# Sending values and keys through DRAM whole, and splitting them where a head loads them

## The chip, the cores and the metric

The kernel runs on one core of a Trainium2 chip. A core has a matrix engine (TensorE, PE in the profile; its weight loads are PEld), a vector engine (VectorE, DVE), an activation engine (ScalarE, ACT), a general engine (GpSimd, POOL) and a queue engine that issues most transfers (SyncE, SP). Each engine works through its own list of instructions in order and waits on semaphores; 16 DMA engines move data between the on-chip memory (SBUF, 128 partitions) and DRAM. Matrix products land in PSUM. The metric is device microseconds of one launch.

## What is computed

Two layers of an encoder with 1024 tokens of width 1024, all in float32. Each layer normalises its input, projects it with one matrix `w_in`, and splits the columns among four groups of four attention heads; their outputs are concatenated, projected with `w_out` and added back; then comes an MLP with squared ReLU.

```python
for l in range(DEPTH):                                  # 2 layers
    h = rms_norm(x, norm1_g[l]);  proj = h @ w_in[l]
    y_a = mla_mixer(...)     # A: 4 heads, dense, latent q and kv, key 64 + 32 rotary
    y_b = diff_mixer(...)    # B: 4 heads, dense, difference of two softmaxes
    y_c = swa_mixer(...)     # C: 4 query heads on 2 key heads, window of +-128 tokens
    y_d = na_mixer(...)      # D: 4 heads, neighbourhood of 8 rows x 16 columns, bias rpb
    x = x + concat(norms of y_a, y_b, y_c, y_d) @ w_out[l]
    x = x + square(relu(rms_norm(x, norm2_g[l]) @ w_up[l])) @ w_down[l]
```

In D the tokens form a grid of 16 rows by 64 columns. A query sees 8 rows and 16 columns around it, and each pair adds a bias from the table `rpb`. All heads have 64 value columns.

## The kernel before

**Precision.** TensorE multiplies the type fp32r. To keep float32 accuracy an operand is held as two fp32r parts: `hi`, a rounded copy that ACT writes (`nc.scalar.activation(hi, src, AF.Copy)`, line L196 in `split`), and `lo = src - hi`, written by DVE or POOL (`tt`, L190). A product then takes several passes over the parts (L222, L223, L224 for the projections).

**Stages of a layer.** `attention` first runs the projections of B in two waves, then four attention stages in the order B, D, C, A. Within a stage `weave` places other products between the attention steps as filler: the projections of A's latents and of D while B runs, the projections of C and A's up-projections (`latent_up`) while D runs, and early parts of the output projection (`groups_bd`) while C and A run. The MLP follows, with a hand-written PE order.

**Through DRAM.** Projected queries, keys and values have tokens and features in the wrong places for attention, so the evacuations store them to DRAM tensors (`keep`, L169, on the SP queue), and each head loads its own (`load`, L162, on SP as well). Before the change every one of these tensors holds both parts. `emit_parts` splits a projected block (ACT copy, subtraction on POOL or DVE) into the tile `both` (two buffers) and stores it; `to_values` transposes a block of values on PE into PSUM, and writes `hi` with ACT (L646) and `lo` with DVE (L190) into `both`. The DRAM tensors are `vb`, `vd`, `vc`, `va` for values (each token row 64 hi and 64 lo), `kd` and `kc` for the keys of D and C (two parts), and others for queries and for the keys of A and B.

**Loading a head.** `vtile` loads one head's values, 512 KB, straight into the tile `v` (two buffers). In `attn_d` a head loads its bias (six blocks of 128 x 128, one buffer), the query parts into one stack tile, and the key parts into two: part hi into both halves of `ks[0]`, part lo into both halves of `ks[1]`, four transfers of 256 KB. `attn_c` does the same once for each of the two key heads. The stack tiles come from the pool `xp` with eight buffers. The softmax tiles `p` (128 x 1024, tag "p") have six buffers (`NP`).

**Attention steps.** For B and A, `softmax` computes scores of a query block (L810), DVE finds the row minimum of the negated scores (L812), ACT exponentiates (L815); B adds the two softmaxes with ACT (L898) and POOL. `dense` transposes the probabilities (L846), splits them (L196, L190 into `pth`, `ptl`) and multiplies with `v` (L834, L835). For D and C, `banded` does the same with blocks of three key tiles: scores L982, `finish` (L1058 and L1061 in D, L1089 and L1092 in C), transposes L991, products L1003 and L1004. `neighbours` builds, once on the host, the index from which a D head's bias blocks are gathered.

**Ending a head.** `denominators` sends the row sums through DRAM (`drows`) and loads them spread over partitions (`rz`); `times` multiplies, and `mix_group` normalises the group and splits it into `mix` tiles, from which the filler `groups_bd` can start. That filler first loads four tiles `sum` of 512 KB.

**What sets the order.** The program text gives priorities (`tc.high_priority`, `weave`); a planner then fixes, before anything runs, one order per engine and the buffer of each tile, from its own estimates of the durations. A change of a load or a buffer can therefore move many neighbouring instructions. At run time each engine keeps that order. SP's transfers use eight semaphores in turn, and in much of the order a transfer waits for the one eight places ahead of it to land.

Of the kernel before, what the change touches and what calls it, by code (L numbers as in the profile page):

```python
# [21 lines left out]
P = 128  # L22
# [56 lines left out]
def neighbours():  # L79
# [8 lines left out]
    out = np.full((P, 6, P), -1)  # L88
    for slot, ok in enumerate((row_ok & (ck >= c), row_ok, row_ok & (ck < c), row_ok, row_ok, row_ok)):
        at = (rk - r + 7) * 31 + 8 * (slot % 3 - 1) + ck - c + 15  # L90
        out[:, slot] = np.where(np.broadcast_to(ok, (P, P)), at, -1)
# [56 lines left out]
class Trunk:  # L148
# [232 lines left out]
    def attention(self, l):  # L381
# [8 lines left out]
        qb, kb, vb = dr([2, 2, 4, 16, 2, S], "qb"), dr([2, 2, 4, 16, 2, S], "kb"), dr([4, P, 8, P], "vb")  # L390
        qd, kd, vd = dr([2, 2, P, S], "qd"), dr([2, 2, P, S], "kd"), dr([4, P, 8, P], "vd")
        qc, kc, vc = dr([2, 2, 2, 32, 2, S], "qc"), dr([2, 2, 32, 2, S], "kc"), dr([2, P, 8, P], "vc")
        lat, krd = dr([2, 3, P, S], "lat"), dr([2, 16, 2, S], "krd")
        qa = dr([2, 2, P, S], "qan"), dr([2, 4, 16, 2, S], "qar")
        ka, va = dr([2, 2, P, S], "kan"), dr([4, P, 8, P], "va")
# [13 lines left out]
        def proj_d():  # L409
            for t in range(2):  # L410
                yield from one(T_DQ[t], xs, self.ev_grid(rb, self.to_parts(qd[:, t], 0.125)))
                yield from one(T_DK[t], xs, self.ev_grid(rb, self.to_parts(kd[:, t])))
# [177 lines left out]
    def ev_rope(self, tabs, dst):  # L590

        dst = dst.rearrange("a g f h s -> a (g f) h s")

        def ev(n, ps):
# [6 lines left out]
            self.tt(t1, t1, t2, ALU.add, self.eng)  # L601
            self.emit_parts(t1, [(dst[:, :, h, sl].rearrange("a p s -> p a s"), slice(h * 64, h * 64 + 64))
# [31 lines left out]

    def to_values(self, dst, tag="mm"):
# [3 lines left out]
        def then(n, y):  # L639
# [3 lines left out]
            src = ps.rearrange("p (k h d) -> p h k d", k=4, h=2)  # L643
            b = self.both()
            v = b.rearrange("p h (k e) -> p h k e", k=4)
            nc.scalar.activation(v[..., 0:64], src, AF.Copy)  # L646
            self.tt(v[..., 64:128], src, v.bitcast(F)[..., 0:64], ALU.subtract)
            self.keep(dst[:, :, n * 4:n * 4 + 4].rearrange("h p k e -> p h (k e)"), b.bitcast(F))
# [143 lines left out]

    def vtile(self, src):
        v = self.ap.tile([P, 8, P], R, tag="v", bufs=2, name="v")
        self.load(v.bitcast(F), src)
        return v
# [238 lines left out]
    def attn_d(self, l, qd, kd, vd, ys):  # L1035
        nc = self.nc
        for t in range(2):
            y, rz = self.ypair(), self.rz_tile()
            for h2 in range(2):
                h = 2 * t + h2  # L1040
                bias = self.ap.tile([P, 6, P], F, tag="bias", bufs=1, name="bias")
# [3 lines left out]
                for i in range(2):  # L1045
                    half = slice(i * 64, (i + 1) * 64)
                    self.load(qs.bitcast(F)[half], qd[i, t, rows])
                    self.load(ks[0].bitcast(F)[half], kd[0, t, rows])
                for i in range(2):
                    self.load(ks[1].bitcast(F)[i * 64:(i + 1) * 64], kd[1, t, rows])  # L1050
# [448 lines left out]
```

## Time and profile before

| | us |
|---|---|
| median of 3 runs | 2708.47 (2705.57 to 2710.37) |
| the profiled execution | 2709.95 |
| its span, first to last instruction | 2707.9 |
| PE busy | 2549.6 (94%) |
| DVE busy | 1943.0 (72%) |
| ACT busy | 1439.8 (53%) |
| POOL busy | 1130.9 (42%) |
| moved by DMA | 389.19 MB, mean 144 GB/s |

The profile page gives one execution, cut into 40 equal slices, with the busy share of each engine, the clock that was granted to TensorE and the share of the DMA engines. The first layer's attention lies between 0 and about 620 us, its MLP up to about 1390 us; the second layer's attention from there to about 1980 us. In layer 0 the first query block of B is exponentiated at 89 us, the first scores of D are at 330 us, and C and A follow until the MLP. Other views used below: the busy time of each engine in chosen stretches, groups of like instructions with their mean duration, who waited for whom, the instructions in order of time, and the chain of work that ended last.

### The profile page before, as it was taken

To read this page: it belongs to the slowest core of one execution; us is meant where nothing else is said; L and a number is where in the kernel's file an instruction comes from. 1 tells how busy PE (TensorE), PEld (TensorE's weight loads), DVE (VectorE), ACT (ScalarE), POOL (GpSimd) and SP (SyncE) were. 2 spreads that over 40 slices of the span, in tenths; PEclk is the share of its full clock that TensorE was granted. 3 is DMA by queue.
4 is the path that set the end of the run, shared out by engine and by line. 5 is a ranking of instruction groups with operands and counts; after the bars stand their busy time and mean duration, and the time that the engine had idled before them with its cause. 6 is when DMAs were issued, how large, how long until landed. Compare 5 with 4: busy or idle time off the path is not lost.

```text
span 2707.9 us, 37502 instructions
## 1 busy us (share of the span) xinstructions
PE 2549.6 (94%) x12296; PEld 2112.5 (78%) x12296; DVE 1943.0 (72%) x3379; ACT 1439.8 (53%) x2601; POOL 1130.9 (42%) x754
## 2 busy tenths in 40 slices
PE   8989988999899998999999999889998999999997
PEld 6778876787778887888877788668876788878886
DVE  6777866774966668887567777677749666688775
ACT  4667756664534444444436776566635344444444
POOL 2555642201345554545434656321013455544442
PEclk9989988999999999999998899899999999999998
DMA  5534597222144457444244446962221444664431
GB/s 175 169 107 129 158 287 239 82 89 63 46 144 148 153 170 267 143 142 141 95 139 134 121 113 183 295 202 69 71 71 52 154 153 152 221 221 146 136 105 63
DMA packets 186931, 389.19 MB, mean 144 GB/s; under 512 B 23712, under 2 KB 26736, under 8 KB 186736
## 3 DMA queue, kind: packets, MB, share of 16 engines
q1 hardware_dynamic: 172912, 361.62, 43.2%
q10 hardware_dynamic: 13824, 25.17, 2.7%
q8 instruction: 97, 1.59, 0.2%
q14 instruction: 98, 0.80, 0.1%
HBM read 263.29 MB, written 123.41 MB: 143 GB/s over the span
## 4 chain that ended last, share of the span: by engine, by line
PE 73%; DVE 12%; DMA 6%; ACT 4%; issue 3%; POOL 1%; SPq 0%; DVEq 0%; ACTq 0%; POOLq 0%
PE u L222 8%; PE u L224 8%; PE u L223 8%; PE mm L222 5%; PE mm L223 5%; PE mm L224 5%; PE p L222 5%; PE p L223 5%; PE p L224 5%; PE sb L810 3%; PE tr L846 3%; DVE p L812 2%; DVE part L190 2%; PE pv L835 2%; PE pv L834 2%
## 5 line engine op out<-in xcount | busy, mean ns | idle before, releaser
L190 POOL TENSOR_TENSOR wl<-raw,wh 128x512 fp32r<-128x512 f32 x448 | 632.8, 1413 | 704.8 <-ACT wh L196 691.0
L196 ACT ACTIVATE wh<-raw 128x512 fp32r<-128x512 f32 x448 | 281.5, 629 | 576.2 <-PE u L223 310.9
L190 POOL TENSOR_TENSOR wl<-ws,wh 128x512 fp32r<-128x512 f32 (+1 forms) x112 | 147.3, 1316 | 461.0 <-ACT wh L196 436.1
L222 PE MATMUL u<-far,wh 128*128 128x512 f32 x768 | 301.8, 393 | 11.4 <-ACT ev L1242 8.3
L224 PE MATMUL u<-far,wl 128*128 128x512 f32 x768 | 300.6, 391 | 2.2 <-POOL wl L190 2.2
L190 DVE TENSOR_TENSOR raw<-raw 128x512 f32<-128x512 f32 x256 | 223.1, 877 | 109.1 <-POOL wl L190 55.6
L223 PE MATMUL u<-far,wh 128*128 128x512 f32 x768 | 300.6, 391 | 0.0
L190 DVE TENSOR_TENSOR ptl<-tr,pth 128x512 fp32r<-128x512 f32 (+2 forms) x384 | 238.3, 629 | 68.5 <-ACT pth L196 66.8
L815 ACT ACTIVATE p<-p,nm 128x1024 f32<-128x1024 f32 x192 | 220.2, 1147 | 92.3 <-DVE nm L812 91.6
L196 ACT ACTIVATE pth<-tr 128x512 fp32r<-128x512 f32 (+2 forms) x384 | 205.2, 546 | 108.5 <-PE tr L846 64.9
L222 PE MATMUL p<-far,wh 128*128 128x512 f32 x640 | 252.9, 395 | 7.5 <-DVE ev L190 7.5
L224 PE MATMUL p<-far,wl 128*128 128x512 f32 x640 | 251.5, 393 | 1.5 <-POOL wl L190 1.5
L223 PE MATMUL p<-far,wh 128*128 128x512 f32 x640 | 252.2, 394 | 0.0
L810 PE MATMUL sb<-stack 96*128 96x512 f32 x640 | 217.5, 422 | 22.1 <-DVE nm L812 21.4
L190 DVE TENSOR_TENSOR far<-act,far 128x512 fp32r<-128x512 f32 x224 | 207.3, 955 | 14.7 <-ACT far L196 14.7
L190 POOL TENSOR_TENSOR p<-p 128x1024 f32<-128x1024 f32 x64 | 154.0, 2411 | 129.6 <-ACT p L898 121.3
L222 PEld LDWEIGHTS u<-far,wh 128*128 128x128 f32 x768 | 145.3, 189 | 43.5 <-ACT ev L1242 9.1
L222 PE MATMUL mm<-xh,wh 128*128 128x512 f32 x416 | 170.9, 411 | 0.8 <-DVE part L190 0.3
L224 PEld LDWEIGHTS u<-far,wl 128*128 128x128 f32 x768 | 145.2, 189 | 33.5 <-POOL wl L190 3.0
L812 DVE CUSTOM_DVE_ANT_0 p<-sb,zero,nm 128x512 f32<-128x512 f32 x192 | 142.4, 743 | 37.7 <-PE sb L810 34.6
L223 PEld LDWEIGHTS u<-far,wh 128*128 128x128 f32 x768 | 145.4, 189 | 30.0
L223 PE MATMUL mm<-xl,wh 128*128 128x512 f32 x416 | 167.7, 403 | 0.0
(245 smaller groups left out, 6110.1 us busy)
## 6 DMA issues: line engine op xcount, KB each, us to landing
act<-acts SPq DMA_DIRECT2D x224, 256.0 KB
raw<-in_w_up SPq DMA_DIRECT2D x128, 256.0 KB
acts<-ev SPq DMA_DIRECT2D x128, 256.0 KB
raw<-in_w_down SPq DMA_DIRECT2D x128, 256.0 KB
acts<-ev ACTq DMA_DIRECT2D x96, 256.0 KB
ws<-in_w_in SPq DMA_DIRECT2D x76, 256.0 KB
rz<-drows SPq DMA_DIRECT2D x40, 256.0 KB
stack<-kd SPq DMA_DIRECT2D x32, 256.0 KB
```

The lines of the kernel that those rows point to most:

```text
L190: (eng or self.nc.vector).tensor_tensor(out=out, in0=a, in1=b, op=op)
L196: nc.scalar.activation(hi, src, AF.Copy)
L222: mm(ps, w[0], x[0][:, sl], start=start, stop=False)
L223: mm(ps, w[0], x[1][:, sl], start=False, stop=False)
L224: mm(ps, w[1], x[0][:, sl], start=False, stop=stop)
L810: self.nc.tensor.matmul(ps, q[:, qt * P:(qt + 1) * P], k[:, sl], start=i == 0, stop=i == len(passes) - 1)
L812: self.nc.vector.tensor_tensor_reduce(out=p[:, sl], in0=ps, in1=self.zero[:, 0:1].bitcast(F).broadcast_to([P, 512]), scale=-scale, scalar= ...
L815: self.nc.scalar.activation(p, p, AF.Exp, bias=nm[:, 1:2], scale=-1.0, accum_out=z)
L834: nc.tensor.matmul(out, v[:, kt], h[:, sl], start=kt == 0, stop=False)
L835: nc.tensor.matmul(out, v[:, kt], lo[:, sl], start=False, stop=kt == 7)
L846: nc.tensor.transpose(t[:, k * 256 + i * P:k * 256 + (i + 1) * P], p[:, (j * 2 + k) * P:(j * 2 + k + 1) * P], self.ident)
```

## The change

Values (`va`, `vb`, `vc`, `vd`) and the keys of D and C (`kd`, `kc`) are stored to DRAM as plain float32, without parts, and each head splits them after loading. `to_values` now writes one tile from the pool "part" (three buffers) with ACT and stores it. `to_whole` stores a D key block as it is, without `both`; `ev_rope` does so for C's keys. `vtile` loads 256 KB into half of a softmax tile `p` and splits it into `v` with ACT and DVE. `split_here` splits a stack tile: ACT writes hi into `ks[0]`, DVE subtracts in place in `ks[1]`, so the two transfers of the other part are gone. A head's bias has five blocks, and the first and last query blocks pick two of them with a stride of two.

```diff
--- before.py
+++ after.py
@@ -85,9 +85,10 @@
     r, c, rk, ck = q // 8, q % 8, k // 8, k % 8
     start = np.clip(r - 4, 0, 8)
     row_ok = (rk >= start) & (rk <= start + 7)
-    out = np.full((P, 6, P), -1)
-    for slot, ok in enumerate((row_ok & (ck >= c), row_ok, row_ok & (ck < c), row_ok, row_ok, row_ok)):
-        at = (rk - r + 7) * 31 + 8 * (slot % 3 - 1) + ck - c + 15
+    out = np.full((P, 5, P), -1)
+    for slot, (off, ok) in enumerate(((-1, row_ok), (-1, row_ok & (ck >= c)), (0, row_ok),
+                                      (1, row_ok & (ck < c)), (1, row_ok))):
+        at = (rk - r + 7) * 31 + 8 * off + ck - c + 15
         out[:, slot] = np.where(np.broadcast_to(ok, (P, P)), at, -1)
     return out
 
@@ -387,12 +388,13 @@
         mix = [None] * 8
 
 
-        qb, kb, vb = dr([2, 2, 4, 16, 2, S], "qb"), dr([2, 2, 4, 16, 2, S], "kb"), dr([4, P, 8, P], "vb")
-        qd, kd, vd = dr([2, 2, P, S], "qd"), dr([2, 2, P, S], "kd"), dr([4, P, 8, P], "vd")
-        qc, kc, vc = dr([2, 2, 2, 32, 2, S], "qc"), dr([2, 2, 32, 2, S], "kc"), dr([2, P, 8, P], "vc")
+
+        qb, kb, vb = dr([2, 2, 4, 16, 2, S], "qb"), dr([2, 2, 4, 16, 2, S], "kb"), dr([4, P, 8, 64], "vb")
+        qd, kd, vd = dr([2, 2, P, S], "qd"), dr([2, P, S], "kd"), dr([4, P, 8, 64], "vd")
+        qc, kc, vc = dr([2, 2, 2, 32, 2, S], "qc"), dr([2, 32, 2, S], "kc"), dr([2, P, 8, 64], "vc")
         lat, krd = dr([2, 3, P, S], "lat"), dr([2, 16, 2, S], "krd")
         qa = dr([2, 2, P, S], "qan"), dr([2, 4, 16, 2, S], "qar")
-        ka, va = dr([2, 2, P, S], "kan"), dr([4, P, 8, P], "va")
+        ka, va = dr([2, 2, P, S], "kan"), dr([4, P, 8, 64], "va")
 
         def evacs_b(t):
             return [self.ev_rope(tabs, qb[:, t]), self.ev_rope(tabs, kb[:, t]),
@@ -409,7 +411,7 @@
         def proj_d():
             for t in range(2):
                 yield from one(T_DQ[t], xs, self.ev_grid(rb, self.to_parts(qd[:, t], 0.125)))
-                yield from one(T_DK[t], xs, self.ev_grid(rb, self.to_parts(kd[:, t])))
+                yield from one(T_DK[t], xs, self.ev_grid(rb, self.to_whole(kd[t])))
                 yield from one(T_DV[t], xs, self.ev_grid(rb, self.to_values(vd[2 * t:2 * t + 2])))
 
         def proj_c():
@@ -589,7 +591,8 @@
 
     def ev_rope(self, tabs, dst):
 
-        dst = dst.rearrange("a g f h s -> a (g f) h s")
+        whole = len(dst.shape) == 4
+        dst = dst.rearrange("g f h s -> (g f) h s" if whole else "a g f h s -> a (g f) h s")
 
         def ev(n, ps):
             sl = slice(n * 512, n * 512 + 512)
@@ -599,6 +602,10 @@
             self.tt(t2[0:64], ps[64:128], s[64:128, sl])
             self.tt(t2[64:128], ps[0:64], s[0:64, sl])
             self.tt(t1, t1, t2, ALU.add, self.eng)
+            if whole:
+                for h in range(2):
+                    self.keep(dst[:, h, sl], t1[h * 64:h * 64 + 64])
+                return
             self.emit_parts(t1, [(dst[:, :, h, sl].rearrange("a p s -> p a s"), slice(h * 64, h * 64 + 64))
                                  for h in range(2)])
         return ev
@@ -632,6 +639,12 @@
             self.emit_parts(y, [(dst[:, :, sl].rearrange("a p s -> p a s"), slice(0, P))], scale=scale)
         return then
 
+    def to_whole(self, dst):
+
+        def then(n, y):
+            self.keep(dst[:, n * 512:n * 512 + 512], y)
+        return then
+
     def to_values(self, dst, tag="mm"):
 
         nc = self.nc
@@ -640,12 +653,11 @@
             ps = self.bank(tag)
             for k in range(4):
                 nc.tensor.transpose(ps[:, k * P:(k + 1) * P], y[:, k * P:(k + 1) * P], self.ident)
-            src = ps.rearrange("p (k h d) -> p h k d", k=4, h=2)
-            b = self.both()
-            v = b.rearrange("p h (k e) -> p h k e", k=4)
-            nc.scalar.activation(v[..., 0:64], src, AF.Copy)
-            self.tt(v[..., 64:128], src, v.bitcast(F)[..., 0:64], ALU.subtract)
-            self.keep(dst[:, :, n * 4:n * 4 + 4].rearrange("h p k e -> p h (k e)"), b.bitcast(F))
+            v = self.part()
+            nc.scalar.activation(v.rearrange("p (h k d) -> p h k d", h=2, k=4),
+                                 ps.rearrange("p (k h d) -> p h k d", k=4, h=2), AF.Copy)
+            self.keep(dst[:, :, n * 4:n * 4 + 4].rearrange("h p k d -> p h (k d)"),
+                      v.rearrange("p (h e) -> p h e", h=2))
         return then
 
     def latent_parts(self, y, g, rows, n, dst, squares):
@@ -790,9 +802,17 @@
     def ptile(self):
         return self.ap.tile([P, S], F, tag="p", bufs=self.NP, name="p")
 
+    def split_here(self, hi, v):
+
+        self.nc.scalar.activation(hi, v.bitcast(F), AF.Copy)
+        self.tt(v, v.bitcast(F), hi.bitcast(F), ALU.subtract)
+
     def vtile(self, src):
+
         v = self.ap.tile([P, 8, P], R, tag="v", bufs=2, name="v")
-        self.load(v.bitcast(F), src)
+        raw = self.ptile()[:, 0:512].rearrange("p (k d) -> p k d", k=8)
+        self.load(raw, src)
+        self.split(v[..., 0:64], v[..., 64:128], raw)
         return v
 
     def transposed(self, w):
@@ -1038,25 +1058,24 @@
             y, rz = self.ypair(), self.rz_tile()
             for h2 in range(2):
                 h = 2 * t + h2
-                bias = self.ap.tile([P, 6, P], F, tag="bias", bufs=1, name="bias")
+                bias = self.ap.tile([P, 5, P], F, tag="bias", bufs=1, name="bias")
                 self.load(bias, self.d["bias"][l, h])
                 qs, ks = self.stack(), [self.stack() for _ in range(2)]
                 rows = slice(h2 * 64, (h2 + 1) * 64)
                 for i in range(2):
                     half = slice(i * 64, (i + 1) * 64)
                     self.load(qs.bitcast(F)[half], qd[i, t, rows])
-                    self.load(ks[0].bitcast(F)[half], kd[0, t, rows])
-                for i in range(2):
-                    self.load(ks[1].bitcast(F)[i * 64:(i + 1) * 64], kd[1, t, rows])
+                    self.load(ks[1].bitcast(F)[half], kd[t, rows])
+                self.split_here(*ks)
                 v = self.vtile(vd[h])
                 z = self.col("z0", 8)
 
                 def finish(ps, p, i):
-                    b0 = {0: 4, 7: 3}.get(i, 0)
-                    w = ps.shape[1]
+                    near = bias[:, {0: slice(2, 5, 2), 7: slice(0, 3, 2)}.get(i, slice(1, 4))]
+                    blocks = lambda t: t.rearrange("p (a b) -> p a b", b=P)
                     nm = self.col("nb")
                     nc.vector.tensor_tensor_reduce(
-                        out=p, in0=ps, in1=bias[:, b0:b0 + w // P].rearrange("p a b -> p (a b)"),
+                        out=blocks(p), in0=blocks(ps), in1=near,
                         scale=-1.0, scalar=3e38, op0=ALU.add, op1=ALU.min, accum_out=nm)
                     nc.scalar.activation(p, p, AF.Exp, bias=nm, scale=-1.0, accum_out=z[:, i:i + 1])
 
@@ -1067,13 +1086,13 @@
 
     def attn_c(self, l, qc, kc, vc, ys):
         nc = self.nc
-        mask = self.ap.tile([P, 6, P], F, tag="bias", bufs=1, name="mask")[:, 0:3]
+        mask = self.ap.tile([P, 5, P], F, tag="bias", bufs=1, name="mask")[:, 0:3]
         self.load(mask, self.d["swa"])
         for kv in range(2):
             ks = [self.stack() for _ in range(2)]
-            for n, k in enumerate(ks):
-                for i in range(2):
-                    self.load(k.bitcast(F)[i * 64:(i + 1) * 64], run(kc[n, kv]))
+            for i in range(2):
+                self.load(ks[1].bitcast(F)[i * 64:(i + 1) * 64], run(kc[kv]))
+            self.split_here(*ks)
             v = self.vtile(vc[kv])
             y, rz = self.big_tile(F, "yc"), self.rz_tile()
             for g in range(2):
```

## The prediction

> **What bounds the kernel now.** I read the page's first parts, then the busy time by stretch, then the waits of PE, then the transfers.
>
> ```profile
> PE 2549.6 (94%) x12296; PEld 2112.5 (78%) x12296; DVE 1943.0 (72%) x3379; ACT 1439.8 (53%) x2601; POOL 1130.9 (42%) x754
> ...
> DMA  5534597222144457444244446962221444664431
> ```
>
> PE is busy 94% of the span. The DMA row has 40 slices of 67.7 us in tenths; it reads 9 in two, the sixth (339 to 406 us) and the 26th (1692 to 1760 us), one in each layer. So the kernel as a whole is bound by PE, and the stages differ.
>
> ```profile
> core 0: us, PE busy (x) PEld busy (x) DVE busy (x) ACT busy (x) POOL busy (x), PEclk, DMA share, GB/s
> 110.00:320.00 210.00, 200.73 (x1091) 169.83 (x1091) 159.27 (x408) 153.71 (x250) 118.36 (x67) 0.97 0.40 117
> 330.00:450.00 120.00, 103.45 (x557) 85.92 (x556) 82.40 (x219) 79.69 (x204) 45.76 (x30) 0.93 0.95 286
> ...
> 1675.00:1795.00 120.00, 98.78 (x530) 82.32 (x528) 77.12 (x203) 75.84 (x194) 43.72 (x29) 0.92 0.97 288
> ...
> 2150.00:2350.00 200.00, 200.00 (x878) 164.66 (x877) 132.89 (x158) 82.62 (x147) 105.28 (x73) 1.00 0.46 154
> ```
>
> The columns are busy microseconds of PE, PEld, DVE, ACT and POOL, the granted clock, the DMA share and GB/s. The MLP stretch (2150 to 2350) is pure PE at full clock, and the change does not touch it. In B (110 to 320) PE is busy 200.73 of 210 us and the DMA engines 40%. Only from the first scores of D into C (330 to 450, and 1675 to 1795 in layer 1) are the DMA engines full: share 0.95 and 0.97, 286 GB/s. There PE is idle 16.55 and 21.22 us, and the clock of 0.93 and 0.92 takes another 0.07 and 0.08 of 120 us, 8.4 and 9.6 us. Both layers together lose 55.8 us. That is all this change can win.
>
> What PE waits for there, layer 0, 330 to 515 us:
>
> ```profile
> PE mm L265 <- DVE sq L190: 3.8, 1, 3.8
> PE pv L1003 <- ACT pth L196: 2.6, 4, 1.5
> PE sb L982 <- DVE nb L1058: 2.2, 1, 2.2
> ...
> PE mm L265 <- DVE part L190: 1.7, 1, 1.7
> ...
> PE mm L223 <- DMA latp<-lat: 1.4, 1, 1.4
> ...
> PE mm L726 <- DMA latp<-lat: 1.1, 2, 0.6
> ...
> PE mm L222 <- DMA latp<-lat: 0.4, 1, 0.4
> ```
>
> The page of these waits sums to 24.4 us in 18 rows; the rows shown carry the argument. Transfers are named for 1.4 + 1.1 + 0.4 us. Two more are transfers behind another engine:
>
> ```profile
> DVE p L1058 <- DMA bias<-in_bias: 6.3, 2, 6.2
> ```
> ```profile
> 357.81 1.97 PE L982 MATMUL sb<-stack 128*128 128x384 f32 x6 [2.25 <-DVE nb L1058]
> ...
> 375.65 3.42 PE L265 MATMUL mm<-pairs,rz 128*128 128x2 f32 x16 [1.72 <-DVE part L190]
> ```
>
> The 2.2 us for DVE's L1058 are the wait for a head's bias, and the 1.7 us before L265 follow the last late load of `latp`. The 3.8 us before the other L265 stand at the end of a chain that begins with a load:
>
> ```profile
> 442.74 7.37 DMA rz<-drows
> ...
> 452.64 1.06 ACT sq L364
> 453.73 1.24 DVE sq L190
> ```
>
> Together 2.9 + 2.2 + 1.7 + 3.8 = 10.6 of 24.4 us, 43%, hang on transfers; the rest on ACT and DVE.
>
> **The change part by part.** First the transfers.
>
> ```profile
> stack<-kd SPq DMA_DIRECT2D x32, 256.0 KB
> ...
> vb<-both SPq DMA_DIRECT2D x8, 512.0 KB
> v<-vb SPq DMA_DIRECT2D x8, 512.0 KB
> ...
> kd<-both SPq DMA_DIRECT2D x8, 512.0 KB
> ...
> stack<-kc SPq DMA_DIRECT2D x16, 256.0 KB
> ...
> bias<-in_bias SPq DMA_DIRECT2D x8, 384.0 KB
> kc<-both SPq DMA_DIRECT2D x8, 256.0 KB
> ...
> sum<-in_x SPq DMA_DIRECT2D x4, 512.0 KB
> ```
>
> There are 28 value loads over both layers (B, D and A four heads, C two, twice), 28 value stores, 32 key loads of D and 16 of C. Each value load and store loses 256 KB: 14 MiB. Half the key loads go: 16 + 8 of 256 KB, 6 MiB. The key stores lose 8 x 256 and 8 x 128 KB, 3 MiB. The bias loses 8 x 64 KB. In all 23.5 MiB. Of this the full stretch of one layer loses three heads' keys of D (6 x 256 KB), C's keys (4 loads, 4 half stores), values of D and C (6 loads), stores of `va` and `vc` (6) and three biases: 6.5 MB, at 286 GB/s 23 us of 120. So the gain is at most 2 x 23 = 45 us, at least nothing, if ACT and DVE take over the waits. I take the share that waits for transfers today: 43% of 55.8 = **-24 us**.
>
> The engines. In the planned order of the changed kernel ACT has 28 instructions more, DVE 12 more and POOL 12 fewer, SP 24 transfers fewer; PE has the same products.
>
> ```profile
> L190 DVE TENSOR_TENSOR raw<-raw 128x512 f32<-128x512 f32 x256 | 223.1, 877 | 109.1 <-POOL wl L190 55.6 <-DMA raw<-in_w_up 51.6
> ...
> L190 POOL TENSOR_TENSOR both<-part,both 128x512 fp32r<-128x512 f32 x48 | 64.3, 1342 | 59.9 <-ACT both L196 40.6 <-DVE nb L1089 11.1 <-DMA ws<-in_w_out 3.2
> ...
> L196 ACT ACTIVATE both<-part 128x512 fp32r<-128x512 f32 x56 | 34.9, 627 | 58.1 <-POOL part L190 29.9 <-DVE part L190 14.6 <-DMA qb<-both 6.8
> ...
> L190 DVE TENSOR_TENSOR sq<-sq 128x1024 f32<-128x1024 f32 x20 | 26.3, 1317 | 9.5 <-ACT sq L364 9.0
> ...
> L364 ACT ACTIVATE sq<-x 128x1024 f32<-128x1024 f32 x16 | 16.1, 1044 | 0.0
> ...
> L190 DVE TENSOR_TENSOR both<-mm,both 128x512 fp32r<-128x512 f32 x20 | 13.6, 685 | 0.9 <-ACT both L646 0.7
> ```
>
> ACT: 28 splits of values at 0.63 us, 12 of keys at 128x1024, nearest 1.04, less 12 copies of 0.63 that went with the key stores: 17.6 + 12.5 - 7.5 = +22.6 us. DVE: the 28 subtractions from PSUM at 0.685 become 28 from two SBUF tiles, at 0.877: +5.4; and 12 of 1.32: +15.8. POOL: 12 x 1.342 = -16.1, worth nothing, since POOL is busy a third of the stretch. In B and A the additions lie beside PE, which has work throughout. Of 40 splits 24 belong to D and C (8 + 4 values, 8 + 4 keys), some 14 us per engine, in stretches where DVE is busy 82.40 of 120 us. That cover is thin where C starts; I take **+4**, between 0 and 14.
>
> The waits that the splits add. A load used to be waited for by PE at the product that needs it; now ACT's copy waits for it, and everything behind it in ACT's list waits too: exponentials, `pth`, the copies `wh` that the filler needs. Behind ACT, DVE waits to subtract. How long ACT waits for a transfer issued shortly before is shown by the stores from `both`:
>
> ```profile
> ACT both L646 <- DMA kb<-both: 14.8, 6, 3.6
> ```
>
> 2.5 us each, 3.6 at most. This row itself shrinks (values leave `both`), but PE had work then, so I give nothing for it.
>
> Where the copies stand in the changed order decides. The worst is the first head of B, at layer 0:
>
> ```profile
> 87.75 0.43 SPq L162 DMA_DIRECT2D stack<-kb  x1
> 88.23 0.42 SPq L162 DMA_DIRECT2D v<-vb  x1
> ```
> ```profile
> 89.16 1.14 ACT L815 ACTIVATE p<-p,nm 128x1024 f32<-128x1024 f32 x1
> ```
> ```profile
> 92.63 0.80 PE L810 MATMUL sb<-stack 96*128 96x512 f32 x1 [2.70 <-DVE nm L812]
> ```
>
> In the changed order its value load comes behind the loads of the second pair (87.75), and ACT's copy stands ahead of the first exponential (89.16). The load cannot be issued before about 88.2, so the first exponential comes at about 92, 3 us late, at a point where PE waits already (2.70 us). I take 3 us per layer, **+6** (0 to 7.4 each, the longest load shown above). The other splits of B and A, 14, stand 3 to 6 us behind their loads in a half idle DMA: nothing, because PE has projections (B) or later scores (A) to do; if that cover is gone, 14 x 2.5 us is the price. The 24 of D and C stand within 2 to 5 us of their loads while DMA is full: 24 x 2.5 = 60 us of waiting on ACT. ACT is idle a third of the stretch anyway, and PE has three score banks and filler; by how much it covers no row tells. I take a quarter, **+15**, between 0 and a half, 30.
>
> A value load now needs a free softmax tile of six, and SP waits for it with everything behind; before, it waited for one of two `v` tiles. The one wait replaces the other: 0. Queue order: the four `sum` loads, 2.1 MB or 7.3 us at 286 GB/s, now precede the last `rz` loads of D, which they followed, in both layers. That is the chain above (rz, times, square, L265). A third of 7.3 us each, **+5**, between 0 and 15, because the transfers ahead of them are shorter. Five bias blocks with a stride: same elements, 0. D's keys now stay in "part" until stored; PE does nothing else for them, 0.
>
> Sum: -24 + 4 + 6 + 15 + 5 = **+6 us**. The profiled execution took 2709.95 us, 1.5 above the median; on the median of 2708.47 this gives 2714.5 us.
>
> One rule is to be weighed. In this trace short gaps cost clock: from 350 to 380 the longest gap of PE is the 2.25 us shown, and then
>
> ```profile
> 370.00:380.00 10.00, 7.67 (x36) 6.78 (x37) 5.67 (x11) 3.81 (x11) 3.67 (x4) 0.79 1.04 319
> ```
>
> with a clock of 0.79. I therefore counted lost clock with idle time. The Trainium skill, "TensorE: Matmul & The Clock Gate", section "HAM oscillation — how this bites in real kernels", gives as the abstract rule that PE must have no idle gaps over about 3.4 us; gaps of 2 us would be free. By it the first term is 43% of 37.8 idle us, -16, and the two waiting terms shrink by a third to +14, so the sum is +7. The trace does not agree with the rule, and the sum hardly depends on it.
>
> **The rivals.**
>
> *The transfers were the bound, and the change is faster: 2685 us.* For it: the DMA share of 0.95 to 0.97 for 120 us, and the chain that runs through loads there. If D and C shrink to the time of their transfers, the first term is -45; with the queue no longer full, the splits of D and C wait half as long, +8, the `rz` loads cost +4, the rest +10: -23. It decides as soon as relief passes the 30 us of the other terms. Against it: 57% of PE's waits there name ACT or DVE, which get more work. The Trainium skill, "DMA: Bandwidth & Descriptors", section "Latency and other measured facts", says that the fixed cost of a transfer falls with lighter memory load, which would help this case; no run here shows it yet.
>
> *ACT's list becomes the bound: 2746 us.* If the 38 splits other than B's first hold ACT 2.5 us and PE sees half, 47 us, the rest as above: -24 + 4 + 6 + 47 + 5 = +38. For it: the rows of 3.6 us. Against: in B PE waits for ACT almost never, 9.3 us idle in 210 for all reasons.
>
> *Nothing to measure: 2708 us.* Half the relief (-12) and half the costs (+15) cancel: +3.
>
> **How the numbers follow.** My forecast, slower by a little, has 0.42, its own range 2709 to 2730; faster 0.37; ACT as bound 0.11; cancelling 0.10. A difference under 0.2% (5.4 us) cannot be told from none here; the forecast lies just above that, so 0.08 of its chance goes to "same". Faster 0.37, same 0.18, slower 0.45. Range: below, the full relief with costs slightly lower still, 2682; above, the ACT case, 2748. Predicted time 2714.
>
> **What would show it.** Right: the DMA share of 330 to 450 clearly under 0.95, PE no longer waiting for `latp`, a new group "ACT v" and "ACT stack" with idle time ended by DMA, the first exponential of B later by 3 us, and PE waits naming ACT `pth` or DVE in D and C larger than 2.6 us. Wrong: PE busy over 110 of 120 us there (faster), or PE waiting in B behind ACT's copies (much slower). A planner that moved fillers in other ways than these lists show would make it wrong without any of them.

## The result, and the profile after

The changed kernel takes 2735.76 us in the median (2733.22 to 2739.53, 4 runs) against 2708.81 for the kernel before (2705.57 to 2710.37, 4 runs on the same chip). The ratio is 1.0102, with a 95% interval of 1.0085 to 1.012: slower by 27 us, where 6 were forecast.

The first rows of the page after, busy time by engine and the share of the DMA engines in 40 slices:

```profile
span 2737.8 us, 37445 instructions
...
PE 2562.3 (94%) x12296; PEld 2108.3 (77%) x12296; DVE 1956.4 (71%) x3391; ACT 1460.4 (53%) x2629; POOL 1118.7 (41%) x742
...
DMA  5433487221234447444244334852221444674431
```

PE is busy 12.7 us longer than before (2549.6) with the same products, and the span is 29.9 us longer. The DMA row falls from 9 to 8 in both full slices, the sixth and the 26th.

The stretches that the prediction took as full, in the changed kernel (busy microseconds of PE, PEld, DVE, ACT and POOL, clock, DMA share, GB/s):

```profile
core 0: us, PE busy (x) PEld busy (x) DVE busy (x) ACT busy (x) POOL busy (x), PEclk, DMA share, GB/s
330.00:450.00 120.00, 98.32 (x532) 80.34 (x530) 85.81 (x209) 81.77 (x190) 48.98 (x31) 0.96 0.86 248
1675.00:1795.00 120.00, 102.28 (x543) 84.58 (x541) 87.18 (x205) 81.24 (x179) 57.79 (x36) 0.93 0.81 235
```

The transfers did get lighter: the share went from 0.95 and 0.97 to 0.86 and 0.81. PE did not profit: together it is busy 200.6 of the 240 us, against 202.2 before.

**Where the time went.** The planner's new order shifts work between stages, so equal times do not compare. I gave each of PE's instructions its undisturbed issue time (that of its kind in these two traces; 0.227 us for a 128x512 product, 2287.6 us in all), summed them in PE's order, and read off when each kernel had done the same sum. (With the tenth percentile or the median of each kind as its time, the entries of these tables move by up to 2.1 us.) The table below has the three places where that differs, as microseconds of the profiled execution above the one of before, both layers together:

| kernel | start of B | D to start of C | C and A | the rest | span |
|---|---|---|---|---|---|
| before, us | 272.2 | 298.8 | 339.8 | 1797.1 | 2707.9 |
| the change | +9.7 | +5.6 | +13.0 | +1.6 | +29.9 |

The same places as windows, before (start of B, D, C and A; then the same of layer 1):

```profile
core 0: us, PE busy (x) PEld busy (x) DVE busy (x) ACT busy (x) POOL busy (x), PEclk, DMA share, GB/s
68.00:179.80 111.80, 99.55 (x477) 80.91 (x476) 85.60 (x186) 71.47 (x118) 66.50 (x38) 0.89 0.51 147
323.70:469.80 146.10, 125.63 (x666) 105.30 (x665) 96.74 (x260) 93.62 (x236) 50.96 (x34) 0.91 0.88 262
469.80:648.20 178.40, 168.37 (x994) 142.05 (x993) 124.22 (x270) 107.76 (x197) 24.85 (x16) 0.99 0.25 71
1358.80:1519.00 160.20, 148.00 (x696) 121.48 (x695) 116.11 (x227) 84.66 (x142) 78.47 (x46) 0.90 0.48 135
1670.30:1823.10 152.80, 127.75 (x682) 106.32 (x681) 101.53 (x269) 98.25 (x249) 54.09 (x34) 0.92 0.87 255
1823.10:1984.60 161.50, 153.55 (x928) 130.92 (x927) 112.58 (x246) 97.56 (x175) 15.76 (x11) 1.00 0.23 67
```

and after:

```profile
67.90:186.40 118.50, 106.26 (x478) 84.84 (x477) 79.88 (x188) 72.90 (x118) 64.89 (x38) 0.86 0.46 127
331.60:482.00 150.40, 122.55 (x666) 99.40 (x665) 110.17 (x271) 104.62 (x250) 54.44 (x33) 0.94 0.77 216
482.00:665.30 183.30, 170.35 (x994) 143.20 (x993) 124.80 (x273) 107.04 (x197) 20.15 (x14) 0.98 0.22 62
1378.70:1542.00 163.30, 148.69 (x696) 119.44 (x696) 112.05 (x228) 87.42 (x146) 77.61 (x46) 0.92 0.43 120
1693.30:1847.40 154.10, 130.44 (x696) 106.64 (x695) 116.32 (x287) 108.78 (x266) 57.54 (x33) 0.92 0.72 211
1847.40:2017.00 169.60, 156.32 (x928) 131.65 (x927) 115.23 (x250) 99.16 (x179) 15.71 (x11) 0.99 0.22 60
```

In C and A the DMA engines are a quarter busy and PE has its whole clock (0.98 to 1.00), yet PE does the same work (994 and 928 products) in 183.3 and 169.6 us instead of 178.4 and 161.5. Nothing there is short of bandwidth. In D of layer 0 the DMA share falls from 0.88 to 0.77 while DVE does 13.4 us more and ACT 11.0, and the stage is no shorter.

**What waits there.** The changed kernel has these waits for transfers (microseconds in all, times, longest), first those of ACT:

```profile
ACT v L197 <- DMA p<-va: 20.5, 7, 4.8
ACT v L197 <- DMA p<-vb: 13.4, 6, 5.5
...
ACT v L197 <- DMA p<-vd: 7.9, 4, 3.2
...
ACT stack L807 <- DMA stack<-kd: 4.9, 3, 2.4
ACT v L197 <- DMA p<-vc: 4.7, 3, 2.2
```

and among those of DVE:

```profile
DVE part L191 <- DMA vb<-part: 17.7, 4, 7.9
```

Neither group is in the profile before, where ACT waited 14.8 us for `both` tiles to be stored. A value block now sits in one of three `part` tiles until `vb` is stored, and the next rotary evacuation on DVE needs that tile. At the start of B in the changed kernel, SP's transfers in order of time (start, duration):

```profile
63.97 0.92 SPq L170 DMA_DIRECT2D vb<-part  x1
...
85.53 0.34 SPq L163 DMA_DIRECT2D p<-vb  x1
```

and DVE's list there, with the idle time before an instruction and what ended it:

```profile
61.36 0.69 DVE L191 TENSOR_TENSOR part<-p,rb 128x512 f32<-128x512 f32 x1
69.13 0.69 DVE L191 TENSOR_TENSOR part<-p,tabc 128x512 f32<-128x512 f32 x1 [7.08 <-DMA vb<-part]
```

DVE stands 7.08 us before this rotary evacuation, until 69.13, 5.2 us after the store of `vb` was issued (63.97). The wait alone loses nothing, though: in the kernel before, the same evacuation starts at 69.22, because DVE there stands behind value copies for which ACT waits until a `both` tile is stored:

```profile
69.22 0.68 DVE L190 TENSOR_TENSOR part<-p,tabc 128x512 f32<-128x512 f32 x1
```

What differs is PE. In the changed kernel's order the first two score products of B stand 56 PE instructions earlier (they start at 72.55 us, before the change at 83.10), and PE waits for their keys (its waits between 50 and 165 us):

```profile
PE sb L830 <- DMA stack<-kb: 2.7, 1, 2.7
```

By equal work PE is 0.1 us behind the kernel before at 68 us, and 4.0 us behind at 80. The projections after it come late, ACT waits for them, and DVE for ACT (ACT's list, then DVE's):

```profile
85.60 0.60 ACT L455 ACTIVATE p<-sb 128x512 f32<-128x512 f32 x1 [6.19 <-PE sb L225]
```

```profile
86.30 0.69 DVE L191 TENSOR_TENSOR part<-p,tabc 128x512 f32<-128x512 f32 x1 [8.92 <-ACT p L455]
```

The row minima stand behind that on DVE, and so the first exponential comes late, in ACT's list:

```profile
89.88 0.64 ACT L197 ACTIVATE v<-p 128x512 fp32r<-128x512 f32 x1 [1.17 <-DMA p<-vb]
...
92.02 1.16 ACT L835 ACTIVATE p<-p,nm 128x1024 f32<-128x1024 f32 x1 [0.59 <-DVE nm L832]
```

The first exponential starts at 92.02, as the prediction had it (92), but not behind the copy of the values (89.88): it waits for DVE's `nm`. The early score products stand in every kernel below that stages B's values in `part` (and in `work`), and in no other one. So the tile brings another order with it, and how much of the loss at the start of B is the wait for a stored tile and how much that order was not separated.

In A it is the other ring. On SP in layer 0, the first fence has the first stack load of A's fourth head and the value load of its third; the second has ACT's list around the copy:

```profile
566.04 0.45 SPq L163 DMA_DIRECT2D stack<-qan  x1
...
570.87 0.34 SPq L163 DMA_DIRECT2D p<-va  x1
```

```profile
571.04 0.60 ACT L197 ACTIVATE pth<-tr 128x512 fp32r<-128x512 f32 x1 [0.82 <-PE tr L866]
575.38 0.63 ACT L197 ACTIVATE v<-p 128x512 fp32r<-128x512 f32 x1 [3.74 <-DMA p<-va]
575.91 1.14 ACT L835 ACTIVATE p<-p,nm 128x1024 f32<-128x1024 f32 x1
```

The value load goes out at 570.87, behind all eight stack loads of the next head (4.83 us behind the first), and ACT stands 3.74 us before the copy; the exponential (L835) starts 4.87 us after the `pth` copy of 571.04. In the kernel before, at the same place, the value load goes out 6.15 us ahead of those stack loads (again SP's transfers, then ACT's list):

```profile
547.35 0.33 SPq L162 DMA_DIRECT2D v<-va  x1
553.50 0.45 SPq L162 DMA_DIRECT2D stack<-qan  x1
```

```profile
558.50 0.60 ACT L196 ACTIVATE pth<-tr 128x512 fp32r<-128x512 f32 x1 [0.82 <-PE tr L846]
561.13 1.15 ACT L815 ACTIVATE p<-p,nm 128x1024 f32<-128x1024 f32 x1 [2.04 <-DVE nm L812]
```

There the exponential starts 2.63 us after the `pth` copy, 2.24 us sooner. If every head of A lost as much, the eight would make 18 us; the stage shows 13.0. The order on SP is the same in both layers: in this kernel and in the three below that load values into a `p` tile and split A's (`vals`, `vals_early`, `vals_both`), the first three heads' value loads stand behind the next head's stack loads; where the load lands in `v`, none stands behind all eight.

### The profile page after: what moved, and what is told of

Read it like the earlier page. It is cut to its first block, busy times and chain, and to the rows that moved or that the text cites. A ratio compares the mean times of both kernels' runs of the same rounds, so it can differ in the third digit from the quotient of the medians.

```text
span 2737.8 us, 37445 instructions
## 1 busy us (share of the span) xinstructions
PE 2562.3 (94%) x12296; PEld 2108.3 (77%) x12296; DVE 1956.4 (71%) x3391; ACT 1460.4 (53%) x2629; POOL 1118.7 (41%) x742
## 5 line engine op out<-in xcount | busy, mean ns | idle before, releaser
L191 POOL TENSOR_TENSOR wl<-ws,wh 128x512 fp32r<-128x512 f32 (+1 forms) x112 | 148.6, 1327 | 458.6 <-ACT wh L197 443.7
L835 ACT ACTIVATE p<-p,nm 128x1024 f32<-128x1024 f32 x192 | 220.0, 1147 | 83.1 <-DVE nm L832 82.0
L830 PE MATMUL sb<-stack 96*128 96x512 f32 x640 | 225.3, 435 | 30.7 <-DVE nm L832 25.5
L225 PE MATMUL mm<-xh,wl 128*128 128x512 f32 x416 | 165.9, 399 | 0.0
```

Of the source, the lines that this page charges most:

```text
L191: (eng or self.nc.vector).tensor_tensor(out=out, in0=a, in1=b, op=op)
L225: mm(ps, w[1], x[0][:, sl], start=False, stop=stop)
L830: self.nc.tensor.matmul(ps, q[:, qt * P:(qt + 1) * P], k[:, sl], start=i == 0, stop=i == len(passes) - 1)
L835: self.nc.scalar.activation(p, p, AF.Exp, bias=nm[:, 1:2], scale=-1.0, accum_out=z)
```

## The experiments

All ratios are to the kernel before on the same chip, with 95% intervals. The table gives the places for each, in the same reading as above; one profiled execution each, and the last columns from the timed runs. A profiled execution can lie off its median (`nolo` 8.1 us above, `vals_inpl` 6.4, the change 3.8), so differences of a few microseconds between two places say little.

| kernel | start of B | D to start of C | C and A | the rest | median us | ratio |
|---|---|---|---|---|---|---|
| the change | +9.7 | +5.6 | +13.0 | +1.6 | 2735.76 | 1.0102 (1.0085 to 1.012) |
| vals | +5.1 | +18.3 | +10.0 | +3.6 | 2745.88 | 1.0134 (1.0113 to 1.0154) |
| keys | +2.3 | +0.7 | -3.2 | +1.6 | 2709.33 | 1.0 (0.9991 to 1.001) |
| bias5 | +0.1 | +6.4 | +3.9 | -4.7 | 2717.78 | 1.0033 (1.0022 to 1.0045) |
| vals_dc | -1.2 | +8.5 | -3.1 | +5.0 | 2714.41 | 1.0021 (1.001 to 1.0032) |
| touch | +5.7 | +6.3 | +5.4 | +0.5 | 2728.97 | 1.0081 (1.0052 to 1.0109) |
| work | +11.9 | -2.8 | +0.5 | +9.1 | 2724.35 | 1.0048 (1.0033 to 1.0064) |
| vals_early | +6.9 | +19.8 | +10.3 | +3.6 | 2748.34 | 1.0147 (1.0125 to 1.0169) |
| vals_both | -1.7 | +22.2 | +7.7 | +7.5 | 2748.33 | 1.0148 (1.0125 to 1.0171) |
| vals_inpl | +26.3 | +12.2 | +1.6 | -6.8 | 2737.08 | 1.0097 (1.0061 to 1.0133) |
| after_i | +15.5 | +2.5 | +1.3 | +2.9 | 2736.99 | 1.0107 (1.0085 to 1.0128) |
| after_ib | +0.7 | +10.7 | +1.2 | -4.2 | 2717.87 | 1.0037 (1.0023 to 1.005) |
| nolo | +0.1 | +1.4 | +2.4 | -2.8 | 2702.57 | 0.9983 (0.997 to 0.9996) |

### The parts of the change alone

Each is the kernel before with one part of the diff. `vals` takes the edits of `to_values`, `vtile` and the four value tensors; `keys` those of `to_whole`, `ev_rope`, `split_here`, `kd` and `kc`; `bias5` the five blocks; `vals_dc` is `vals` for `vd` and `vc` alone.

> Only the values go whole, in all four groups; keys and bias as before. Three theories. (W) the loss is ACT waiting for value loads and DVE waiting for `part` tiles held by value stores: nearly all of the loss is here, 2728 to 2740 us. (E) the loss is the added work on ACT and DVE: 28 splits add 28 x 0.63 us on ACT, about half of what the whole change adds, so about half of the loss, 2718 to 2725. (P) the planner's new order alone makes the difference, whatever is edited: 2710 to 2735, with no relation to the other parts.

> Only the keys of D and C go whole; values and bias as before. (W): few loads are waited for (5.5 us of ACT in the changed kernel), 24 loads and 16 half stores less: 2700 to 2711 us. (E): 12 splits of 1.05 us on ACT and 1.48 us on DVE, half of the added work: 2718 to 2725. (P): 2710 to 2735, with no relation to bytes or work.

> Only the bias tile of five blocks. No work added, 64 KB less for each of eight heads. (W) and (E): 2706 to 2711 us. (P): if the planner's order moves with it, a difference of 5 us and more either way, which would be the size of its accident.

> Only the values of D and C go whole, where the transfers are full; B and A, the keys and the bias as before. (W) as far as the waits are those of B and A (33.9 of 46.6 us of ACT's waiting, and all of the 17.7 us for `vb`): 2706 to 2716 us. (E): 12 of 40 splits: 2714 to 2718. (P): anything from 2705 to 2735. If the transfers were worth something in D and C, below 2706.

`vals` alone is slower than the whole change, and than all three expected: 2745.88 us. `keys` costs and gains nothing, 2709.33, though it takes 24 loads and 16 half stores away and adds 12 splits. `vals_dc` costs 5.6 us. So the loss is with the values, and by the totals over 30 us of it with those of B and A. The places do not agree: of the 37 us of `vals`, 18.3 lie in D, where `vals_dc` has 8.5, and 15.1 at the start of B and in C and A. This speaks for waits (W) against work in proportion (E), by which `keys` should have cost as much as the values; but `keys` also takes transfers away, so its zero may hold a cost and a gain of like size. It also shows the size of accident (P): five bias blocks add no work and lie 9 us above before, 1.0033; the parts sum to 46 us and the whole is 27.

```diff
 # vals, vals_dc: for all four groups, or for d and c alone
-vb = dr([4, P, 8, P], "vb"); to_values and vtile with parts
+vb = dr([4, P, 8, 64], "vb"); to_values and vtile as in the change
 # keys
-kd = dr([2, 2, P, S], "kd"); kc = dr([2, 2, 32, 2, S], "kc")
+kd = dr([2, P, S], "kd"); kc = dr([2, 32, 2, S], "kc"); split_here, to_whole
 # bias5
-bias = self.ap.tile([P, 6, P], F, tag="bias", bufs=1, name="bias")
+bias = self.ap.tile([P, 5, P], F, tag="bias", bufs=1, name="bias")
```

### Work at the loads, without the rings

The kernel before, its bytes and rings untouched, with ACT and DVE passing over a head's values where they land:

```diff
         self.load(v.bitcast(F), src)
+        hi, lo = v[..., 0:64], v[..., 64:128]
+        self.nc.scalar.activation(hi, hi.bitcast(F), AF.Copy)
+        self.tt(lo, lo.bitcast(F), hi.bitcast(F), ALU.bypass)
         return v
```

> The kernel before (parts through DRAM, all bytes as before), with the 28 splits' work added at the place where a head's values land: ACT rewrites the hi part in place, DVE passes over the lo part in place. No `p` tile, no `part` tile, no byte changes. (W1) if ACT and DVE waiting for the value loads, with what stands behind them, is the loss of the values: 2728 to 2745 us, as the run with the values alone (2746). (W2) if the loss is the `part` tiles held by value stores or the `p` tile taken by the load: 2706 to 2716. (P) the planner's order by itself: up to 9 us above before, as the bias alone gave.

2728.97 us, +0.81%, at the lower edge of (W1); (W2) and (P) are refuted. The splits behind a load do cost without the two rings, spread over the three places (+5.7, +6.3, +5.4). ACT waits 26 us for the loads here.

Whether that is the work or the wait was to be told apart by the same work behind no load:

```diff
         self.load(v.bitcast(F), src)
+        one = self.zero[:, 0:1].bitcast(F).broadcast_to([P, 64])
+        for _ in range(3):
+            a, b = (self.ap.tile([P, 64], F, tag="wk" + n, bufs=1, name="wk" + n) for n in "ab")
+            self.nc.scalar.activation(a, one, AF.Copy)
+            self.tt(b, one, a, ALU.subtract)
         return v
```

> The kernel before, with about the 28 splits' work on ACT and DVE (three small passes each, on a constant) at the same places in the program, but behind no load. (E) if the work itself is what the splits cost: 2722 to 2735 us, as the run that touches the loaded values (2729). (W1) if it is the wait for the load, with the rest of the list behind it: 2705 to 2716.

This edit did not do what it says. Waiting for nothing, all passes were planned to the start of a layer (the last of the 84 starts at 1413.7 us), where the kernel loses 11.3 us (layer 1) and some 8 (layer 0, in "the rest"), and nothing in D, C and A. Its 2724.35 us lies in (E)'s range and answers nothing on the splits; how much of `touch` is work and how much is wait stays open.

### The two rings

`vals_early` writes a head's `vtile` ahead of its other loads. `vals_both` and `vals_inpl` start from `vals` and put back one ring each:

```diff
 # vals_early, for B (and likewise in A, D and C)
             y, rz = pair["y"], pair["rz"]
+            v = self.vtile(vb[2 * t + h2])
             qk = []
...
-            v = self.vtile(vb[2 * t + h2])
 # vals_both, in to_values
-            v = self.part()
+            v = self.both().bitcast(F)[:, 0]
 # vals_inpl, in vtile
-        raw = self.ptile()[:, 0:512].rearrange("p (k d) -> p k d", k=8)
-        self.load(raw, src)
-        self.split(v[..., 0:64], v[..., 64:128], raw)
+        hi, lo = v[..., 0:64], v[..., 64:128]
+        self.load(lo.bitcast(F), src)
+        self.nc.scalar.activation(hi, lo.bitcast(F), AF.Copy)
+        self.tt(lo, lo.bitcast(F), hi.bitcast(F), ALU.subtract)
```

> Values alone, with a head's value load and split written ahead of its query and key loads in every group, so that the load is issued earlier against the first exponential and ACT's copy does not stand behind the last load of the head. (W1): ACT's waits for values (55 us in the run with the values alone) fall to half or less, and the time to 2715 to 2732 us. (p) and (W2): as without it or worse, 2737 to 2755, since a `p` tile is held longer.

> Values alone, but `to_values` stages a block in the tile `both` (two buffers, as before the change) in place of `part` (three). (W2, `part`): DVE no longer waits for `vb` and `va` stores (22 us in the run with the values alone), 10 us and more come back: 2725 to 2736 us. (W1) and (p): no change beyond the planner's accident, 2737 to 2750.

> Values alone, but the load lands in the lo half of the tile `v` itself (pieces of 256 bytes) and is split in place: no `p` tile is taken. (p) if the loss is that a value load waits for a softmax tile and takes one of six: 2712 to 2730 us. (W1) the copy waits for the load all the same: 2737 to 2750, more if the short pieces make the load slower.

Written earlier, the load is not issued earlier: the first is at 87.1 us, 85.5 without the edit, the second at 149.0 (148.6), released by POOL's work on a softmax tile. So its place in the program does not set it; the second points to the tile. By total time `vals_both` looks like nothing and `vals_inpl` like 9 us, and what (W2) and (p) expected of them was missed. By place each does what its theory says, and no more: with `both` the start of B falls from +5.1 to -1.7, with the load in `v` the stage C and A falls from +10.0 to +1.6. What they win is lost elsewhere: `vals_both` has +22.2 in D, and `vals_inpl` +26.3 at the start of B, where ACT's copies now stand earlier and wait up to 7.0 us for the loads of `vb` (22.0 us in all); that these are late because the stores are was not tried.

So both were put back in the changed kernel, and one of them alone:

> The changed kernel with two edits: the value load lands in the lo half of `v` and is split there (no `p` tile), and `to_values` stages in `both` (DVE does not wait for `part`). (p and `part`) if these two rings are what the change costs beyond the splits: 2712 to 2724 us. (W1) alone: 2728 to 2740. Better than before (below 2700) only if the relief is worth what the prediction gave it.

> The changed kernel with one of the two edits alone: the value load lands in the lo half of `v`, so that it takes no softmax tile; `to_values` stages in `part` as in the change. (p) if the softmax tile is what counts: as with both edits, 2713 to 2724 us. (`part`) if the wait of DVE for stored `part` tiles counts as much: 2725 to 2738, with the 17.7 us of DVE's waits for `vb` stores still there.

With both, 2717.87 us: two thirds of the loss is gone. The start of B is at +0.7 and C and A at +1.2. With the load in `v` alone, 2736.99, as slow as the change: C and A is right (+1.3), and the start of B is worse (+15.5). The waits of ACT, then of DVE, in `after_i`:

```profile
ACT v L815 <- DMA v<-vb: 17.9, 5, 6.0
...
ACT v L815 <- DMA v<-va: 4.1, 5, 1.5
```

```profile
DVE part L191 <- DMA vb<-part: 16.7, 4, 8.6
```

and those of ACT in `after_ib`, where DVE has no wait for a `part` tile left:

```profile
ACT v L815 <- DMA v<-vb: 10.5, 5, 2.7
...
ACT v L815 <- DMA v<-va: 2.7, 4, 1.2
```

The expectation that the softmax tile alone would decide fell. For C and A the tile is what counts: from +7.7 to +13.0 in the four kernels that load A's values into `p`, from +1.2 to +1.6 in the three that load them raw into `v` (`touch`, which splits there too with all bytes, has +5.4). At the start of B, `both` for `part` took 6.8 us away in one pair of kernels and 14.8 in the other, each time with the other planned order as well. In `after_ib`, C and A take what they took before (windows of the two layers, columns as above):

```profile
475.30:654.00 178.70, 167.94 (x994) 141.16 (x994) 125.92 (x274) 107.38 (x200) 20.25 (x14) 1.00 0.23 63
...
1832.80:1995.10 162.30, 153.87 (x928) 130.68 (x927) 114.81 (x249) 98.54 (x178) 15.77 (x11) 1.00 0.22 61
```

### The relief alone

The kernel before, without the transfers of the keys' lo part in D and C:

```diff
 # attn_d, and likewise in attn_c
-                qs, ks = self.stack(), [self.stack() for _ in range(2)]
+                qs, ks = self.stack(), [self.stack()] * 2
...
-                for i in range(2):
-                    self.load(ks[1].bitcast(F)[i * 64:(i + 1) * 64], kd[1, t, rows])
```

> The kernel before, with the transfers of the keys' lo part in D and C left out (12 loads of 256 KB per layer, 3.1 MB) and no work added: the products take the hi part a second time, so the lo part of the keys is missing from the result; PE has the same products. This is the relief alone. (R) if transfers bound the full stretches as the prediction had it, 11 us per layer times 43% or more: 2688 to 2700 us. (N) if PE there waits for DVE and ACT, which the relief does not touch: 2703 to 2712, or an accident of the planner.

2702.57 us, 0.9983 (0.997 to 0.9996): a gain of 4.6 us, between 1 and 8 (6.4 between the medians), where the prediction's reading wanted 9.5 at least (43% of 22). In the profiled execution, the slowest of the ten, D is 8.8 us faster in layer 0 and 10.2 slower in layer 1. Its two windows of D, columns as above:

```profile
324.20:461.50 137.30, 119.04 (x669) 98.92 (x668) 97.46 (x260) 94.07 (x237) 50.94 (x34) 0.95 0.84 255
1661.30:1824.20 162.90, 136.60 (x682) 113.47 (x680) 102.62 (x267) 97.48 (x248) 54.44 (x35) 0.85 0.76 220
```

Fewer bytes (255 and 220 GB/s, against 262 and 255), nearly the same work on DVE and ACT, and in layer 1 a clock of 0.85. The same edit in the same stage gives both signs, some 10 us each way. That the planner's order makes the difference is likely, since `bias5` moves by as much without any work, but the order was not held fixed in any run, so it is not shown. The +5.6 us of the change in D lies within this accident, and its cause stays open.

Taken together the table says a little more of D. All nine kernels that split D's values show a loss there, 2.5 to 22.2 us and 11.8 in the mean; the four others have 1.4 in the mean. So the value splits seem to cost in D; no single run shows it clear of the accident.

## Why the prediction was right, and where it was not

The sign and the range held; the size did not, and 2735.76 us lies above the forecast's own range of 2709 to 2730. That the sign came out is in part luck: the terms set for D and C cancel in the sum (-24 + 4 + 15 + 5 = 0), and the two places that lost most were priced at +6 and at nothing. Step by step:

- **Relief, -24: the measure failed, the size stays open.** It was the share of PE's waits in the full stretches that ended in a transfer. `nolo`, the one run with relief alone, takes away 6 of the 23.5 MiB and gains 4.6 us, half of the 9.5 that this reading wanted at least. The waits that it counted did not all go: PE waits 4.4 us for `latp` between 331 and 482 us in the changed kernel, and waited 2.9 in the prediction's rows. What the whole relief is worth no run tells, since every other one adds splits. `touch`, with the value splits and all bytes, costs 22.6 us, and `after_ib`, with all splits and the bytes gone, 8.9; but by place that difference is not in D (+6.3 against +10.7), where the transfers were full. The rival that forecast 2685 us has this term at its largest and missed by 51 us.
- **ACT and DVE, +4:** the counts and durations were right or close. The groups of the splits in the changed kernel (busy, mean ns, idle before):

```profile
L191 DVE TENSOR_TENSOR v<-p,v 128x512 fp32r<-128x512 f32 x28 | 20.7, 738 | 32.0 <-ACT v L197 31.8
...
L191 DVE TENSOR_TENSOR stack<-stack 128x1024 fp32r<-128x1024 f32 x12 | 17.8, 1481 | 6.0 <-ACT stack L807 6.0
L197 ACT ACTIVATE v<-p 128x512 fp32r<-128x512 f32 x28 | 17.6, 627 | 46.6 <-DMA p<-va 20.5 <-DMA p<-vb 13.4 <-DMA p<-vd 7.9
...
L807 ACT ACTIVATE stack<-stack 128x1024 fp32r<-128x1024 f32 x12 | 12.6, 1052 | 8.2 <-DMA stack<-kd 4.9 <-PE sb L830 2.8 <-DMA stack<-kc 0.6
```

The copies took 0.627 and 1.052 us (0.63 and 1.04 forecast), the subtractions 0.738 (0.877) and 1.481 (1.32). What they cost in D can't be told from the accident in any one kernel.
- **First head of B, +6: the time was right for another reason.** The first exponential of layer 0 moved by 2.86 us as forecast, but the value load was out at 85.53, ahead of the 88.2 that the prediction had as the earliest, and the exponential stood behind DVE. The place lost 9.7 us over both layers, and 9.0 of it came back in `after_ib`, where `to_values` no longer uses `part`, and nothing in `after_i`, where it does. The prediction gave `part` a zero ("PE does nothing else for them") and looked at the keys of D alone; the values of B were what it held. Whether they cost by the wait or by the order planned around it is open.
- **ACT held in D and C, +15: the wait was too large.** The rows above give 7.9 + 4.7 us for the values, 4.9 for the keys of D and 0.6 for those of C: 18.1 us of ACT's waiting over 24 splits, 0.75 us each, not 2.5. What PE lost by it was not measured.
- **The softmax tile, 0: failed, and by place the largest miss.** "The one wait replaces the other" compared the waits of SP, and not when they end. The program has two `v` tiles, and one is free when the head before last is done; the six `p` tiles go round among the softmaxes of the head that still runs, and the load goes out behind the next head's stack loads and not ahead of them. In A the prediction also trusted later scores as cover. ACT waits 20.5 us there for the values, and with the load back in `v` (`after_i`) 11.7 of the 13.0 us of that stage return.
- **`rz` behind the `sum` loads, +5: fell.** PE's wait for the squares behind that chain was 3.8 us in one case; in the changed kernel it is 0.8 in all (waits of PE):

```profile
PE mm L266 <- DVE sq L191: 0.8, 2, 0.4
```

- **ACT's list as the bound, 2746:** the mechanism is the nearest to what happened (the exponentials of A stand behind a copy), but there it starts from a ring, and the copies of D and C waited far less than 2.5 us.

By place, the gap between +6 and the 29.9 us of the profiled span is 13.0 us in C and A (forecast: nothing for the softmax tile), 5.6 in D (where the terms cancelled), 3.7 at the start of B (9.7 against 6) and 1.6 elsewhere. That the costs were +30 in the sum, as much as the span grew, is chance: 13.0 and 9.7 us of the growth sit where a ring was set to 0.

## What to carry to other kernels

When a transfer is made smaller by splitting later, follow the buffers and not only the bytes: a raw copy needs a tile between load and split, and another until its store has landed, and whoever shares those rings can pay. Compare when a load can be issued before and after, from the release of its tile. Do not price a relief by the waits that name a transfer. Do not price a wait by its length alone either: look whether the same instruction started sooner before. Where a planner makes the order, compare places at equal work, not totals alone: here totals hid two effects of 9 and 12 us behind shifts of 10 us, and an edit without added work (`bias5`) moved the total by as much.

## What was not expected of the hardware

Transfers at a share of 0.95 to 0.97 and 286 GB/s held PE less than that share suggests: 3.1 MB less per layer gained 4.6 us in all (1 to 8). And the granted clock falls without longer gaps: at the start of B in layer 0 the changed kernel has a clock of 0.86 against 0.89 with the same idle time of PE (12.2 us each: 118.5 - 106.26, and 111.8 - 99.55) and a shorter longest gap (3.5 against 4.6 us), and the 6.7 us lost there are all in slower products. In layer 1 it is the other way: 3.1 us lost with a clock of 0.92 against 0.90 and 2.4 us more idle time. A store of 256 KB held its tile 5.2 us, and DVE waited up to 7.9 us for one, twice the longest such wait that the prediction had found (3.6).
